# Attention's output weights loaded ahead in two DMAs each, and other loads moved later

## The chip, the cores and the metric

The kernel runs on one core of a Trainium2 chip. The metric is the device time of one execution in microseconds. Of the kernel before, three runs gave 2224.09, 2224.7 and 2230.74 us, a median of 2224.7 us. Engines are called TensorE (PE), VectorE (DVE), ScalarE (ACT), GpSimd (POOL) and SyncE (SP, whose queue issues all the DMAs spoken of here).

## The reference

One layer of a hybrid encoder over 2048 tokens of width 1024, in float32:

```python
h = rms_norm(x, norm1)
z = h @ w_in                       # q: 8 heads, k and v: 2 heads of 64, u: 512 columns
att = windowed_gqa(q, k, v, ...)   # QK norm, window of +-128 tokens, ALiBi, a sink logit per head
ssm = s5_mixer(u, ...)             # bidirectional complex diagonal scan, 32 groups; then GELU and GLU
x = x + concat([att, ssm]) @ w_out
x = x + square(relu(rms_norm(x, norm2) @ w_ff1)) @ w_ff2
```

`w_out` has 1024 rows. The upper 512 multiply the attention's result, and only these are loaded by the lines that the change touches. Attention works on blocks of 128 queries, each against its own block of keys and its two neighbours.

## The kernel before

Matrix products that need more precision are made of three: each operand is split into a rounded part and a rest (`woh` and `wol` for the output weights, `ah` and `al` for attention's result), and high x high, high x low and low x high are summed. So each weight tile needs a DMA into a raw tile, a copy on ScalarE that rounds it (L990), and a subtraction on VectorE (L991).

The program has these stages: (a) norm, transposes and the product for u, to about 139 us; (b) the products for q and k, v (`pq`, `pk`, in 16 tiles of 128 tokens, in pairs whose transposed inputs `hh` and `hl` are loaded by L898); (c) attention from about 349 to 720 us; (d) GLU, output projection of the state space part, second norm; (e) the two feed-forward products, from about 960 us on. Beside (b) and (c) runs the state space work as a second stream of steps (`ssm_stream`), in 8 sets of 4 groups: `ssm_load` brings a set's input `u` in 16 DMAs (L572), `pair_in` multiplies it (`ptv`, `pvu`), `ssm_rotate`, `ssm_scan` and `ssm_unrotate` work on VectorE, `pair_out` makes a kernel table that goes out to memory (`ks` to `kd_dr`, L738 and L740) and comes back in another layout (`tt`, L747), and `pair_y` multiplies with it (`py`, L759 and L762). How many of its steps follow each step of the main stream is set by a fixed rate (`Side`).

After each tile of (b), the keys are transposed (`ptk`, L944), scaled and split into `k_hh` and `k_ll` (`late_k`, L946 and L947). These calls wait in a list `late` until the next tile is under way. The order of the tiles is 14, 15, 12, 13, 0 to 11, so the last two calls, for tiles 10 and 11, are made when (b) has ended, ahead of attention.

Attention has 32 units: a block of 128 queries by one of the two key heads. `front(u)` makes a unit's queries (`q_prep`: `ptq`, `qs`), scores (`pss`) and softmax; `back(u)`, three units later (LEAD = 3), transposes the probabilities (`ptp`, copied to `pT` by L1061), multiplies with v (`pv`) once per block, splits the result (`ah` L1075, `al` L1076) and makes the output product of the block before (`poa`). `load_wo` is called twice in each of the units 1 to 4 and does DMA, rounding and subtraction for one of 8 parts: head `hh` of the four in a group, and a half of the columns. A part's 128 partitions are 64 rows for each key head, so the source of its one DMA has the two key heads outermost. Its raw tile `woraw` shares 7 buffers with `pT`.

A scheduler puts each engine's instructions into a fixed order from the program's order, the dependences and its own model of times. An engine then works strictly in that order, and SyncE issues its DMAs so too: a DMA that waits for something holds up all that stand behind it.

Of the kernel before, what the change touches and what calls it, by code (L numbers as in the profile page):

```python
# [11 lines left out]
F32 = mybir.dt.float32  # L12
# [8 lines left out]
P = 128  # L21
# [5 lines left out]
NKV = 2  # L27
GQ = 4
HD = 64
AW = 512  # L30
# [14 lines left out]
PTB = 7  # L45
# [12 lines left out]
def hymba_kernel(ctx: ExitStack, tc: tile.TileContext, x, norm1, w_in, q_gain, k_gain, sink,  # L58
                 lam_re, lam_im, log_dt, b_re, b_im, c_re, c_im, d_skip, w_glu, w_out,
                 norm2, w_ff1, w_ff2, out):  # L60
    nc = tc.nc
# [504 lines left out]
    def ssm_load(i):  # L566
        u = pm2.tile([P, 4, NC_], F32, tag="u", name="u")
        for g in range(4):
            for q in range(4):
                src = u_dr[q, (4 * i + g) * GH:(4 * i + g + 1) * GH]  # L570
                rows = bass.AP(src.tensor, src.offset, [[64, T], [T * 64, GH], [1, 64]])
                nc.sync.dma_start(out=u[:, g, q * 64:(q + 1) * 64], in_=rows)  # L572
        st[i] = {"u": u}
# [197 lines left out]
    NB4 = NG // 4  # L771

    def ssm_stream():
        ssm_load(0)
        yield from pair_in(0, 0)
        yield from pair_in(0, 1)
        yield from ssm_tables(0)
        for i in range(NB4):
            if i + 1 < NB4:
                ssm_load(i + 1)  # L780
            yield from ssm_rotate(i)
            yield from pair_out(i, 0)
            yield from ssm_scan(i)
            yield from ssm_unrotate(i)
            yield from pair_y(i, 0)
            if i + 1 < NB4:
                yield from pair_in(i + 1, 0)
            yield from pair_out(i, 1)
            if i + 1 < NB4:
                yield from pair_in(i + 1, 1)  # L790
                yield from ssm_tables(i + 1)
            else:
                for _ in range(8):
                    yield
            yield from pair_y(i, 1)
            del st[i]
# [84 lines left out]
    side = Side(side_stream(), SIDE_STEPS, SIDE_MAIN)  # L881


    with tc.tile_pool(name="p1", bufs=2) as p1:
        gq = p1.tile([P, 2], F32, name="gq", bufs=1)
        for j, gain in enumerate((q_gain, k_gain)):
            for r in range(2):
                nc.sync.dma_start(out=gq[r * HD:(r + 1) * HD, j:j + 1], in_=gain.rearrange("o d -> d o"))
        DVE.tensor_tensor(gq[:, 0:1], gq[:, 0:1], gq[:, 1:2], op=ALU.mult)
        hsc = p1.tile([P, 10], F32, name="hsc", bufs=1)  # L890
        DVE.memset(hsc, 1.0)
        for h in range(NH):
            DVE.memset(hsc[:, h:h + 1], -1.0 / (SLOPE[h] * math.sqrt(HD)))

        def load_h(b):
            for j, v in enumerate(ht_tiles(b)):
                for t in range(2):
                    nc.sync.dma_start(out=v.bitcast(F32)[:, :, t * P:(t + 1) * P],  # L898
                                      in_=ht_dr[2 * b + t, j].rearrange("p (k t) -> p k t", k=KD))

        def qkv_part(t):
            hh, hl = (a[:, :, (t % 2) * P:(t % 2) * P + P] for a in ht[t // 2])
            pq = ps.tile([P, 512], F32, tag="sc", name="pq")
            pk = ps.tile([P, 256], F32, tag="mm", name="pk")
            for k in range(KD):
                mm3(pq, hh[:, k, :], hl[:, k, :], wqh[:, k, 0:512], wql[:, k, 0:512], k == 0, k == KD - 1)
                yield 0.65
            for k in range(KD):
                mm3(pk, hh[:, k, :], hl[:, k, :], wqh[:, k, 512:768], wql[:, k, 512:768], k == 0, k == KD - 1)
                if k % 2:  # L910
                    yield 0.65
            pq3 = pq.rearrange("p (h d) -> p h d", d=HD)
            pk3 = pk[:, 0:128].rearrange("p (h d) -> p h d", d=HD)
            sq = p1.tile([P, 10, HD], F32, tag="sq", name="sq", bufs=1)
            ACT.activation(out=sq[:, 0:8], in_=pq3, func=AF.Square)
            ACT.activation(out=sq[:, 8:10], in_=pk3, func=AF.Square)
            ACT.activation(out=v_all[:, t, :], in_=pk[:, 128:256], func=AF.Copy)
            ms = p1.tile([P, 10], F32, tag="msq", name="msq")
            rs = p1.tile([P, 10], F32, tag="rsq", name="rsq")
            t3 = p1.tile([P, 10], F32, tag="t3", name="t3")  # L920
            DVE.tensor_reduce(ms, sq, axis=AX.X, op=ALU.add)
            DVE.tensor_scalar(ms, ms, 1.0 / HD, EPS, op0=ALU.mult, op1=ALU.add)
            ACT.activation(out=rs, in_=ms, func=AF.Sqrt)
            DVE.reciprocal(rs, rs)
            DVE.tensor_tensor(t3, rs, rs, op=ALU.mult)
            DVE.tensor_tensor(t3, t3, ms, op=ALU.mult)
            DVE.tensor_scalar(t3, t3, -0.5, 1.5, op0=ALU.mult, op1=ALU.add)
            DVE.tensor_tensor(rs, rs, hsc, op=ALU.mult)
            DVE.tensor_tensor(rs, rs, t3, op=ALU.mult)
            yield 0.0  # L930
            rs3 = rs.rearrange("p (h o) -> p h o", o=1)
            DVE.tensor_tensor(sq[:, 0:8], pq3, rs3[:, 0:8].to_broadcast([P, 8, HD]), op=ALU.mult)
            qd = p1.tile([P, NH, 2, HD], F32R, tag="qd", name="qd", bufs=1)
            kd = p1.tile([P, 2, 2, HD], F32, tag="kd", name="kd", bufs=3)
            for r in range(2):
                DVE.tensor_tensor(kd[:, :, r, :], pk3, rs3[:, 8:10].to_broadcast([P, 2, HD]), op=ALU.mult)
            ACT.activation(out=qd[:, :, 0, :], in_=sq[:, 0:8], func=AF.Copy)
            DVE.tensor_tensor(qd[:, :, 1, :], sq[:, 0:8], qd[:, :, 0, :], op=ALU.subtract)
            nc.sync.dma_start(out=q_dr[t], in_=qd.bitcast(F32).rearrange("p h r d -> p (h r d)"))

            def late_k():
                pt = ps.tile([P, 2, P], F32, tag="tr", name="ptk")
                for kv in range(2):
                    nc.tensor.transpose(pt[:, kv, :], kd[:, kv].rearrange("p r d -> p (r d)"), ident)  # L944
                ts_ = slice(t * P, (t + 1) * P)
                ACT.activation(out=k_hh[:, :, ts_], in_=pt, func=AF.Copy, scale=gq[:, 0:1])  # L946
                DVE.scalar_tensor_tensor(k_ll[:, :, ts_], pt, gq[:, 0:1], k_hh[:, :, ts_],  # L947
                                         op0=ALU.mult, op1=ALU.subtract)

            late.append(late_k)  # L950

        late = []
        order = [NB - 1, NB - 2] + list(range(NB - 2))
        for i, b in enumerate(order):
            for t in (2 * b, 2 * b + 1):
                if t % 2 == 0 and 1 <= i < NB - 1:
                    load_h(order[i + 1])
                for j, c in enumerate(qkv_part(t)):
                    side.step(c * FIRST)
                    if j == 4 and len(late) > 1:  # L960
                        late.pop(0)()
        while late:
            late.pop(0)()
    hstack.close()
    wqkv.close()

# [1 line left out]
    with tc.tile_pool(name="pbq", bufs=2) as pbq, tc.tile_pool(name="pb", bufs=1) as pb, \  # L968
# [4 lines left out]
        def load_q(n):  # L973
            qt = pbq.tile([P, NH, P], F32R, tag="qraw", name="qraw")
            nc.sync.dma_start(out=qt.bitcast(F32), in_=q_dr[n].rearrange("p (h r) -> p h r", h=NH))
            q_raw[n] = qt

        nc.sync.dma_start(out=nsink, in_=sink[0:1, :].to_broadcast([P, NH]))
        DVE.tensor_scalar(nsink, nsink, -1.0, None, op0=ALU.mult)
        load_q(0)  # L980
        load_q(1)
        woh = pb.tile([P, GQ, D], F32R, name="woh")
        wol = pb.tile([P, GQ, D], F32R, name="wol")

        def load_wo(hh, half):
            cs = slice(half * 512, half * 512 + 512)
            raw = pb.tile([P, 512], F32, tag="pT", name="woraw", bufs=PTB)
            src = w_out[0, 0:AW, cs].rearrange("(g hh d) n -> hh g d n", g=NKV, hh=GQ)
            nc.sync.dma_start(out=raw, in_=src[hh])
            ACT.activation(out=woh[:, hh, cs], in_=raw, func=AF.Copy)  # L990
            DVE.tensor_tensor(wol[:, hh, cs], raw, woh[:, hh, cs], op=ALU.subtract)  # L991

# [104 lines left out]
            yield 0.65  # L1097

        wo_parts = [(hh, half) for half in range(2) for hh in range(GQ)]

        def front(u):

            n, g = divmod(u, 2)
            for h in range(GQ):
                scores(n, g, h)
                if h == GQ - 1:
                    softmax(n, g)
                yield 0.33
                if h % 2 and u > 0 and wo_parts:
                    load_wo(*wo_parts.pop(0))  # L1110
                if h == 1 and u + 1 < 2 * NT:
                    q_prep(*divmod(u + 1, 2))
                    if g == 0 and n + 2 < NT:
                        load_q(n + 2)
                    yield 0.44
# [448 lines left out]
```

## Time and profile before

| | us |
|---|---|
| median of three runs | 2224.7 |
| the profiled execution, its own time | 2234.64 |
| its span | 2232.9 |
| TensorE busy | 2084.3 (93%) |
| VectorE busy | 1478.7 (66%) |
| ScalarE busy | 1016.1 (46%) |
| GpSimd busy | 591.5 (26%) |

TensorE is busy nearly throughout, so time is lost where it is not, or where its granted clock is below 1. The page's 40 slices of 55.8 us show three such places: the seventh slice (335 to 391 us, the change from stage (b) to attention), the seventeenth (893 to 949 us, the output projection) and the twenty-ninth (1563 to 1619 us, the change to the second feed-forward product). The DMA engines move 151 GB/s on average.

### The profile page before, as it was taken

How to read it: one execution, taken by the hardware profiler on the slowest of the kernel's cores; microseconds unless marked ns; L12 is line 12 of the kernel's file. 1: busy time of each engine (PE TensorE's matmuls, PEld its weight loads, DVE VectorE, ACT ScalarE, POOL GpSimd, SP SyncE). 2: the span in 40 equal slices, each digit the busy share in tenths (PEclk: the TensorE clock that was granted, in tenths of full speed). 3: DMA queues.
4: the chain of work that ended last, by engine and by line, in shares of the span. 5: the costliest groups of instructions: out<-in, count | busy, mean ns of one | idle time of the engine just before them, and what ended most of it. 6: DMA issues, size and time to landing. Idle time of an engine off the chain costs nothing.

```text
span 2232.9 us, 30461 instructions
## 1 busy us (share of the span) xinstructions
PE 2084.3 (93%) x10546; PEld 1710.8 (77%) x10546; DVE 1478.7 (66%) x2806; ACT 1016.1 (46%) x2061; POOL 591.5 (26%) x451
## 2 busy tenths in 40 slices
PE   7999995899999998699999999999599999999999
PEld 7888884677776776588888788888477787778787
DVE  7869876788775644565555655554677767776765
ACT  4433324677666532455555655555332332333331
POOL 2000000000002223232222122222554653663541
PEclk9999997999999999699999999999799999999999
DMA  9834543233326355844444644443573443443334
GB/s 257 284 90 135 158 127 110 90 107 102 109 83 184 118 203 193 274 154 153 156 156 156 217 156 156 154 149 112 199 242 115 128 131 101 128 128 107 125 130 163
DMA packets 284154, 337.06 MB, mean 151 GB/s; under 512 B 62688, under 2 KB 211168, under 8 KB 284000
## 3 DMA queue, kind: packets, MB, share of 16 engines
q1 hardware_dynamic: 284000, 335.12, 46.3%
q8 instruction: 83, 1.36, 0.3%
q14 instruction: 71, 0.58, 0.1%
HBM read 206.11 MB, written 128.94 MB: 150 GB/s over the span
## 4 chain that ended last, share of the span: by engine, by line
PE 63%; DVE 15%; DMA 8%; POOL 5%; issue 4%; ACT 3%; SPq 2%; DVEq 0%; POOLq 0%; ACTq 0%
PE f L87 6%; PE f L89 6%; PE f L88 6%; PE f_al L87 5%; PE f_al L89 5%; PE f_al L88 5%; POOL w2s L1452 3%; PE f_ga L89 2%; PE f_ga L87 2%; PE f_ga L88 2%; POOL fs L1478 1%; PE pv L1069 1%; DMA woraw<-in_w_out_dram 1%; DVE acc L1523 1%; PE f_be L88 1%
## 5 line engine op out<-in xcount | busy, mean ns | idle before, releaser
L1523 DVE TENSOR_TENSOR acc<-f,acc 128x512 f32<-128x512 f32 x448 | 304.9, 687 | 162.0 <-PE f L89 155.3
L87 PE MATMUL f<-w2s,fs 128*128 128x512 f32 x896 | 352.3, 393 | 30.5 <-DVE acc L1523 15.9
L89 PE MATMUL f<-w2s,fs 128*128 128x512 f32 x896 | 350.2, 391 | 4.9 <-POOL fs L1478 4.9
L88 PE MATMUL f<-w2s,fs 128*128 128x512 f32 x896 | 349.9, 391 | 0.0
L1477 ACT ACTIVATE fs<-fr 128x512 fp32r<-128x512 f32 x224 | 141.6, 633 | 363.1 <-PE f L89 344.9
L1478 POOL TENSOR_TENSOR fs<-fr,fs 128x512 fp32r<-128x512 f32 x128 | 185.4, 1451 | 295.8 <-ACT fs L1477 247.8
L87 PEld LDWEIGHTS f<-w2s,fs 128*128 128x128 f32 x896 | 169.0, 189 | 73.7 <-ACT fs L1477 26.3
L1321 POOL TENSOR_TENSOR w1s<-w1r,w1s 128x512 fp32r<-128x512 f32 x96 | 135.4, 1411 | 310.6 <-ACT w1s L1320 305.1
L87 PE MATMUL f_al<-hb,w1s 128*128 128x512 f32 x512 | 201.0, 393 | 0.7 <-ACT w1s L1320 0.7
L89 PE MATMUL f_al<-hb,w1s 128*128 128x512 f32 x512 | 200.7, 392 | 0.9 <-DVE w1s L1321 0.8
L88 PE MATMUL f_al<-hb,w1s 128*128 128x512 f32 x512 | 200.4, 392 | 0.0
L89 PEld LDWEIGHTS f<-w2s,fs 128*128 128x128 f32 x896 | 168.9, 189 | 41.1 <-POOL fs L1478 5.6
L88 PEld LDWEIGHTS f<-w2s,fs 128*128 128x128 f32 x896 | 169.1, 189 | 34.4
L818 POOL TENSOR_TENSOR wgl<-wgr,wgh 128x512 fp32r<-128x512 f32 x8 | 10.4, 1317 | 555.2 <-DMA wgr<-in_w_glu_dram 542.4
L1321 DVE TENSOR_TENSOR w1s<-w1c,w1s 128x512 fp32r<-128x512 f32 x96 | 68.3, 711 | 87.9 <-ACT w1s L1320 87.9
L89 PEld LDWEIGHTS f_al<-hb,w1s 128*128 128x128 f32 x512 | 96.5, 189 | 21.9 <-DVE w1s L1321 1.2
L87 PEld LDWEIGHTS f_al<-hb,w1s 128*128 128x128 f32 x512 | 96.7, 189 | 21.0 <-ACT w1s L1320 1.1
L88 PEld LDWEIGHTS f_al<-hb,w1s 128*128 128x128 f32 x512 | 96.6, 189 | 19.5
L1320 ACT ACTIVATE w1s<-w1c 128x512 fp32r<-128x512 f32 x128 | 80.6, 630 | 49.6 <-PE f_al L89 48.4
L88 PE MATMUL f_ga<-hb,w1s 128*128 128x512 f32 x256 | 99.9, 390 | 0.0
L87 PE MATMUL f_ga<-hb,w1s 128*128 128x512 f32 x256 | 99.8, 390 | 0.0
L89 PE MATMUL f_ga<-hb,w1s 128*128 128x512 f32 x256 | 99.7, 389 | 0.0
(548 smaller groups left out, 4975.3 us busy)
## 6 DMA issues: line engine op xcount, KB each, us to landing
fr<-f_dr SPq DMA_DIRECT2D x224, 256.0 KB
w1r<-in_w_ff_dram SPq DMA_DIRECT2D x64, 512.0 KB
f_dr<-fs SPq DMA_DIRECT2D x128, 256.0 KB
f_dr<-f SPq DMA_DIRECT2D x96, 256.0 KB
w2r<-in_w_ff_dram SPq DMA_DIRECT2D x32, 512.0 KB
hs<-hc_dr SPq DMA_DIRECT2D x56, 256.0 KB
xt<-in_x_dram SPq DMA_DIRECT2D x16, 512.0 KB
q_dr<-qd SPq DMA_DIRECT2D x16, 512.0 KB
```

The source lines that it names most:

```text
L87: nc.tensor.matmul(ps_ap, lhsT=lh, rhs=rh, start=first, stop=False, skip_group_check=onto)
L88: nc.tensor.matmul(ps_ap, lhsT=lh, rhs=rl, start=False, stop=False, skip_group_check=onto)
L89: nc.tensor.matmul(ps_ap, lhsT=ll, rhs=rh, start=False, stop=last, skip_group_check=onto)
L818: eng_lo.tensor_tensor(lo, raw, hi, op=ALU.subtract)
L1069: nc.tensor.matmul(po[g * HD:(g + 1) * HD, :], lhsT=v_all[:, lo + kt, g * HD:(g + 1) * HD], rhs=pT.pop((n, g, kt)), start=kt == 0, stop=kt ...
L1320: ACT.activation(out=t[:, 0], in_=src, func=AF.Copy)
L1321: (DVE if m in (6, 7, 3) else POOL).tensor_tensor(t[:, 1], src, t[:, 0], op=SUB)
L1452: (DVE if m in (6, 7, 3) and fp else POOL).tensor_tensor(t[:, 1], src, t[:, 0], op=SUB)
L1477: ACT.activation(out=t[:, 0], in_=src, func=AF.Copy)
L1478: (DVE if m in (6, 7, 3) else POOL).tensor_tensor(t[:, 1], src, t[:, 0], op=SUB)
L1523: DVE.tensor_tensor(a[:, cs], po, a[:, cs], op=ADD)
```

## The change

The diff, whole:

```diff
--- before.py
+++ after.py
@@ -776,11 +776,11 @@
         yield from pair_in(0, 1)
         yield from ssm_tables(0)
         for i in range(NB4):
-            if i + 1 < NB4:
-                ssm_load(i + 1)
             yield from ssm_rotate(i)
             yield from pair_out(i, 0)
             yield from ssm_scan(i)
+            if i + 1 < NB4:
+                ssm_load(i + 1)
             yield from ssm_unrotate(i)
             yield from pair_y(i, 0)
             if i + 1 < NB4:
@@ -881,8 +881,11 @@
     side = Side(side_stream(), SIDE_STEPS, SIDE_MAIN)
 
 
+    late_stack = ExitStack()
+    with tc.using_default_side("right"):
+        lk = late_stack.enter_context(tc.tile_pool(name="lk", bufs=1))
     with tc.tile_pool(name="p1", bufs=2) as p1:
-        gq = p1.tile([P, 2], F32, name="gq", bufs=1)
+        gq = lk.tile([P, 2], F32, name="gq")
         for j, gain in enumerate((q_gain, k_gain)):
             for r in range(2):
                 nc.sync.dma_start(out=gq[r * HD:(r + 1) * HD, j:j + 1], in_=gain.rearrange("o d -> d o"))
@@ -931,7 +934,7 @@
             rs3 = rs.rearrange("p (h o) -> p h o", o=1)
             DVE.tensor_tensor(sq[:, 0:8], pq3, rs3[:, 0:8].to_broadcast([P, 8, HD]), op=ALU.mult)
             qd = p1.tile([P, NH, 2, HD], F32R, tag="qd", name="qd", bufs=1)
-            kd = p1.tile([P, 2, 2, HD], F32, tag="kd", name="kd", bufs=3)
+            kd = lk.tile([P, 2, 2, HD], F32, tag="kd", name="kd", bufs=3)
             for r in range(2):
                 DVE.tensor_tensor(kd[:, :, r, :], pk3, rs3[:, 8:10].to_broadcast([P, 2, HD]), op=ALU.mult)
             ACT.activation(out=qd[:, :, 0, :], in_=sq[:, 0:8], func=AF.Copy)
@@ -959,8 +962,6 @@
                     side.step(c * FIRST)
                     if j == 4 and len(late) > 1:
                         late.pop(0)()
-        while late:
-            late.pop(0)()
     hstack.close()
     wqkv.close()
 
@@ -975,18 +976,23 @@
             nc.sync.dma_start(out=qt.bitcast(F32), in_=q_dr[n].rearrange("p (h r) -> p h r", h=NH))
             q_raw[n] = qt
 
+        load_q(0)
         nc.sync.dma_start(out=nsink, in_=sink[0:1, :].to_broadcast([P, NH]))
         DVE.tensor_scalar(nsink, nsink, -1.0, None, op0=ALU.mult)
-        load_q(0)
-        load_q(1)
         woh = pb.tile([P, GQ, D], F32R, name="woh")
         wol = pb.tile([P, GQ, D], F32R, name="wol")
 
+        wo_raw = {}
+
         def load_wo(hh, half):
-            cs = slice(half * 512, half * 512 + 512)
             raw = pb.tile([P, 512], F32, tag="pT", name="woraw", bufs=PTB)
-            src = w_out[0, 0:AW, cs].rearrange("(g hh d) n -> hh g d n", g=NKV, hh=GQ)
-            nc.sync.dma_start(out=raw, in_=src[hh])
+            src = w_out[0, 0:AW, half * 512:half * 512 + 512].rearrange("(g hh d) n -> hh g d n", g=NKV, hh=GQ)
+            for g in range(NKV):
+                nc.sync.dma_start(out=raw[g * HD:(g + 1) * HD], in_=src[hh][g])
+            wo_raw[hh, half] = raw
+
+        def split_wo(hh, half):
+            raw, cs = wo_raw.pop((hh, half)), slice(half * 512, half * 512 + 512)
             ACT.activation(out=woh[:, hh, cs], in_=raw, func=AF.Copy)
             DVE.tensor_tensor(wol[:, hh, cs], raw, woh[:, hh, cs], op=ALU.subtract)
 
@@ -1097,6 +1103,12 @@
             yield 0.65
 
         wo_parts = [(hh, half) for half in range(2) for hh in range(GQ)]
+        for part in wo_parts[:4]:
+            load_wo(*part)
+        load_q(1)
+        for part in wo_parts[4:PTB]:
+            load_wo(*part)
+        late_wo = wo_parts[PTB:]
 
         def front(u):
 
@@ -1106,8 +1118,14 @@
                 if h == GQ - 1:
                     softmax(n, g)
                 yield 0.33
-                if h % 2 and u > 0 and wo_parts:
-                    load_wo(*wo_parts.pop(0))
+                if h % 2 and u > 1 and wo_parts:
+                    split_wo(*wo_parts.pop(0))
+                    if late_wo:
+                        load_wo(*late_wo.pop(0))
+                if h == 2 and u > 0 and late:
+                    late.pop(0)()
+                    if not late:
+                        late_stack.close()
                 if h == 1 and u + 1 < 2 * NT:
                     q_prep(*divmod(u + 1, 2))
                     if g == 0 and n + 2 < NT:
```

It has these parts.

1. `load_wo` only issues DMAs now, two for each part (64 partitions each, one per key head). Seven parts, as many as there are buffers, are asked for ahead of unit 0, the eighth after the first split.
2. `split_wo` does the rounding and the subtraction, twice in each of the units 2 to 5 instead of 1 to 4.
3. The last two `late_k` are made in units 1 and 2 of attention. What they read (`kd` and the gains `gq`) moves into a pool of its own that lives until then.
4. `ssm_load` of the next set is called after `ssm_scan` instead of ahead of `ssm_rotate`.
5. `load_q(0)` stands ahead of the sink's load, and `load_q(1)` between the fourth and the fifth weight part.

What the scheduler makes of it: the orders differ from the first of the `u` loads (139 us in the trace) to the last third of attention; from there to the end all engines have the same order as before.

SyncE at the start of attention, before (`tt`: the state space table, `qraw`: a block's queries, `xr`: the input rows for the residual):

```order
L747 DMA tt<-kd_dr 128x1x384
L975 DMA qraw<-q_dr 128x1024
L989 DMA woraw<-in_w_out_dram 128x1x512 x3
L975 DMA qraw<-q_dr 128x1024
L989 DMA woraw<-in_w_out_dram 128x1x512
L1084 DMA xr<-in_x_dram 128x1024
L989 DMA woraw<-in_w_out_dram 128x1x512 x4
L975 DMA qraw<-q_dr 128x1024
```

and now:

```order
L747 DMA tt<-kd_dr 128x1x384 x2
L976 DMA qraw<-q_dr 128x1024
L991 DMA woraw<-in_w_out_dram 64x512 x16
L976 DMA qraw<-q_dr 128x1024
L1090 DMA xr<-in_x_dram 128x1024
L976 DMA qraw<-q_dr 128x1024
```

The first weight DMA stands at the same place, behind the third block of queries; the eight are now sixteen, without a gap, and the fourth block of queries and `xr` come behind all of them. The last two of the sixteen wait for the first split's buffer.

SyncE in the state space work of the second set, while the third set's `u` is loaded (`y_dr`: a result stored, `hh`, `hl`: inputs of the next pair of tiles, `kd_dr`: the table stored), before:

```order
L768 DMA y_dr<-ys 8x16x256 x2
L572 DMA u<-u_dr 128x1x64 x16
L898 DMA hh<-ht_dr 128x8x128 x2
L939 DMA q_dr<-qd 128x1024
L898 DMA hl<-ht_dr 128x8x128 x2
L738 DMA kd_dr<-ks 16x256
L740 DMA kd_dr<-ks 16x240
L738 DMA kd_dr<-ks 16x256
L740 DMA kd_dr<-ks 16x240
L747 DMA tt<-kd_dr 128x1x384
```

and now:

```order
L768 DMA y_dr<-ys 8x16x256 x2
L572 DMA u<-u_dr 128x1x64 x7
L901 DMA hh<-ht_dr 128x8x128 x2
L901 DMA hl<-ht_dr 128x8x128 x2
L738 DMA kd_dr<-ks 16x256
L740 DMA kd_dr<-ks 16x240
L942 DMA q_dr<-qd 128x1024
L738 DMA kd_dr<-ks 16x256
L740 DMA kd_dr<-ks 16x240
L747 DMA tt<-kd_dr 128x1x384
L572 DMA u<-u_dr 128x1x64 x3
L747 DMA tt<-kd_dr 128x1x384
```

Nine of the sixteen `u` loads have moved from ahead of the table's stores to behind its first reload, and a store of queries stands between the table's stores.

TensorE at the start of attention, before (`pkd`: the state space table's product):

```order
L726 MATMUL pkd<-q_n,f_i_1814 32x256 x2
L730 MATMUL pkd<-c_r,bb_r 16x16 x2
L730 MATMUL pkd<-c_n,bb_i 16x16 x2
L944 MATMUL ptk<-ident,kd 128x128 x4
L1008 MATMUL ptq<-ident,qraw 128x128 x5
L1023 MATMUL pss<-k_hh,qs 128x256
```

and now:

```order
L726 MATMUL pkd<-q_n,f_i_1814 32x256 x2
L730 MATMUL pkd<-c_r,bb_r 16x16 x2
L730 MATMUL pkd<-c_n,bb_i 16x16 x2
L1014 MATMUL ptq<-ident,qraw 128x128 x8
L1029 MATMUL pss<-k_hh,qs 128x256
```

The four key transposes ahead of the first query transposes are gone; two of them now stand behind the scores of the first unit and two among the scores of the third.

## Rows read from the trace of the kernel before

**Rows 1.** The page: span, and TensorE's granted clock in 40 slices, in tenths.
```profile
span 2232.9 us, 30461 instructions
...
PEclk9999997999999999699999999999799999999999
```
**Rows 2.** Stretches of the opening: length, PE, PEld, DVE, ACT, POOL busy, PEclk, DMA share, GB/s.
```profile
371.00:413.00 42.00, 18.29 (x89) 12.48 (x90) 17.47 (x52) 19.28 (x51) 0.00 (x0) 0.67 0.23 76
356.70:406.20 49.50, 24.51 (x108) 17.12 (x109) 22.11 (x80) 25.11 (x65) 0.00 (x0) 0.67 0.32 99
356.70:368.50 11.80, 11.56 (x62) 9.82 (x63) 6.28 (x32) 6.89 (x16) 0.00 (x0) 0.78 0.52 143
413.00:443.00 30.00, 28.03 (x181) 22.60 (x182) 29.55 (x82) 24.78 (x70) 0.00 (x0) 1.00 0.31 92
```
**Rows 3.** Chain of work that ended last, in order of time: start, length, what.
```profile
378.38 15.45 DMA woraw<-in_w_out_dram
...
395.23 15.01 DMA woraw<-in_w_out_dram
```
**Rows 4.** Waits, 345 to 420 us: who waited for whom, us in total, times, longest.
```profile
ACT woh L990 <- DMA woraw<-in_w_out_dram: 22.6, 8, 4.7
...
PE ptq L1008 <- ACT pT L1061: 17.1, 1, 17.1
```
**Rows 5.** ScalarE's groups, 356.7 to 406.2 us: busy, mean ns, idle before them.
```profile
L990 ACT ACTIVATE woh<-woraw 128x512 fp32r<-128x512 f32 x7 | 4.4, 629 | 18.5 <-DMA woraw<-in_w_out_dram 18.5
L1010 ACT ACTIVATE qs<-ptq 128x512 fp32r<-128x512 f32 x6 | 3.6, 595 | 5.3 <-PE ptq L1008 4.5 <-PE pss L1024 0.8
```
**Rows 6.** DMA engines from 378 to 388 us, in 40 slices of 0.25 us.
```profile
DMA  1111935699944111111111111111111111101111
GB/s 49 49 49 49 279 98 180 229 360 393 377 180 180 49 49 49 49 49 49 49 49 49 49 49 49 49 49 49 49 49 49 49 49 49 66 33 66 49 49 41
```
**Rows 7.** The opening in order of time: start, length, engine, instruction, idle before it.
```profile
348.43 0.33 SPq L975 DMA_DIRECT2D qraw<-q_dr  x1
...
355.17 0.66 PE L944 MATMUL ptk<-ident,kd 128*128 128x128 f32 x2 [5.32 <-DVE kd L936]
...
356.72 0.60 ACT L1010 ACTIVATE qs<-ptq 128x512 fp32r<-128x512 f32 x1 [0.38 <-PE ptq L1008]
...
361.12 4.46 SPq L989 DMA_DIRECT2D woraw<-in_w_out_dram  x3
...
405.56 0.59 ACT L1075 ACTIVATE ah<-pv 128x512 fp32r<-128x512 f32 x1
...
413.33 0.48 PE L87 MATMUL poa<-woh,ah 128*128 128x512 f32 x1
```
**Rows 8.** SyncE's queue in the state space groups, in order of time.
```profile
208.24 9.81 SPq L572 DMA_DIRECT2D u<-u_dr  x16
...
223.63 2.25 SPq L738 DMA_DIRECT2D kd_dr<-ks  x1
...
229.33 0.62 SPq L747 DMA_DIRECT2D tt<-kd_dr  x1
...
284.09 0.62 SPq L747 DMA_DIRECT2D tt<-kd_dr  x1
```
**Rows 9.** TensorE in the same two groups.
```profile
229.81 1.06 PE L637 MATMUL pvu<-u,vt 128*128 128x128 f32 x8
...
233.71 0.71 PE L759 MATMUL py<-u,tt 128*128 128x128 f32 x4 [1.47 <-DMA tt<-kd_dr]
...
288.49 1.22 PE L759 MATMUL py<-u,tt 128*128 128x128 f32 x4 [4.00 <-DMA tt<-kd_dr]
```
**Rows 10.** Two stretches of the second group, columns as in rows 2.
```profile
280.00:290.00 10.00, 5.79 (x34) 4.96 (x33) 4.47 (x14) 2.85 (x7) 0.00 (x0) 0.84 0.53 155
290.00:300.00 10.00, 10.00 (x67) 9.22 (x68) 4.86 (x8) 1.41 (x4) 0.00 (x0) 0.82 0.13 36
```
**Rows 11.** Issues on SyncE by tile: least, median and longest ns, first and last start.
```profile
L572 SPq DMA_DIRECT2D u<-u_dr x128: 567/574/707, 139.2 to 559.2; - x128
```

## The prediction, made before the changed kernel was run

> **What bounds the kernel now.** I read the page first, then the opening of attention in stretches, then the chain of waits, the waits by engine, the DMA rate, and last SyncE's queue in the state space work. The page gives a span of 2232.9 us, and TensorE is busy for most of it; one of the three places where its granted clock is below full level is the seventh slice, where attention begins [rows 1]. There TensorE is busy for only 18.29 of the 42 us from 371 to 413, at a mean clock of 0.67, a mixture of the two levels of 1.2 and 2.4 GHz, and from 413 on it is busy for 28.03 of 30 at 1.00 [rows 2]. So some 24 us are lost in this one stretch, and nothing in it is bound by an engine: ScalarE has 19.28 us of work, VectorE 17.47.
>
> The chain of waits names what ends last there: two pieces of about 15 us each are DMAs of `woraw` [rows 3]. ScalarE, which works strictly in its order, waits for them 8 times, 22.6 us in all; while it stands before one rounding, the copies of transposed probabilities queue behind it, and TensorE waits 17.1 us for one of these [rows 4]. Of the 22.6 us, 18.5 fall ahead of `ah`, the first split result of attention [rows 5], and 4.1 between `ah` at 405.56 and the first output product at 413.33 [rows 7].
>
> Why are the loads so slow? In most slices where only they run, the engines move 49 GB/s and are busy for one tenth; when `xr` joins, the same engines reach 393 GB/s [rows 6]. One part is 128 rows of 2 KB, 262 KB, and 262 KB / 49 GB/s = 5.3 us. So a part's DMA uses about a tenth of the engines; its source has the two key heads outermost, and the DMA that runs beside it has not.
>
> **The weights (parts 1 and 2 of the change).** The same eight roundings and eight subtractions are made; only what ScalarE waits for goes. The first weight DMA keeps its place behind the third block of queries, at 361.1 before [rows 7], some 3 us earlier now (next part). Sixteen issues at the median of a `u` issue, 0.574 us [rows 11], are 9.2 us, so the seventh part is issued by about 366. A transfer of 131 KB at 180 to 393 GB/s [rows 6] takes 0.3 to 0.7 us, about an issue, and from issue to use I allow the 4.4 us that `tt` took (229.33 to 233.71) [rows 8, 9]. All seven parts are there by 371. The first rounding now stands behind the second unit's exponentials, and ScalarE was through the first unit's only at about 368.5, so none of the seven is waited for. The eighth waits for the first subtraction; behind it SyncE holds the fourth block of queries and `xr`, both first used more than 15 us later. Taken away: 22.6 us.
>
> What comes late instead? ScalarE's order, and what feeds it. From the first `qs` at 356.72 to `ah` it has 25.11 us of work in 49.5 [rows 2]; without the 18.5 us it would need 31. Work added to it there: the two `k_hh` copies, at most 0.6 us each, since `qs` with twice the columns takes 0.595 [rows 5]: +1.2. Waits that surface: between 368.5 and 406.2 its work is 25.11 - 6.89 = 18.2 us. At the pace of the first 11.80 us, in which no weights are waited for (4.91 us idle on 6.89 of work), this would bring 13 us of waits; at the pace of 413 to 443 (5.22 on 24.78) 3.8; with perfect overlap none [rows 2]. I take 4, since the stretch has the same mixture of two units at work as the steady state. VectorE, with 22.11 us in the opening, has room.
>
> A rule speaks against splitting the DMA. The Trainium skill (DMA: Bandwidth & Descriptors, section Rules for kernel authors) says that two transfers to disjoint halves of the partitions are not worth it, since both run over all 16 engines and serialize. By it the split would bring nothing, which is a rival below. The same page (section Why a DMA increments its semaphore by 16 and not by 1) lets the number of engines be the largest up to 16 that divides the slowest dimension of both sides: 2 for the old source, 16 for each of the new ones, and the sum would be as here. The trace's tenth of the engines is nearer to the second.
>
> **The key transposes (part 3).** TensorE's first query transposes stand behind those of the last tile, which wait 5.32 us for VectorE's `kd` [rows 7]. Now they stand first and wait for their own data, asked for at 348.43. With 4.4 us from issue to use they start at 352.8 instead of 355.6: -2.8. Ends: 0, if the queries land later than that, and -5.3, the whole wait. The scores of block 0 read neither tile; the moved transposes take places in units 1 and 2, where TensorE waits anyway.
>
> **The state space loads (part 4).** The third set's 16 `u` issues hold SyncE from 208.24 for 9.81 us; the table's store follows at 223.63 and its reload at 229.33 [rows 8]. TensorE waits 1.47 us for that table, and 4.00 us for the next set's at 288.49 [rows 9], after which its clock is 0.84 and 0.82 over 20 us [rows 10]. Nine issues fewer ahead of the table are 9 x 0.574 = 5.2 us. Best end: both waits (5.5) and what the clock lost (0.16 + 0.18 of 10 us each, 3.4): -8.9. Worst end: TensorE's order has also moved `py` ahead, by up to 8 us, and a query store stands between the table's stores, so a new wait of 3 us is possible: +3. I take -3, the middle: the larger wait goes, and a smaller new one comes in another set.
>
> **Clock.** The output products now start while TensorE has just been half idle; before, it had been busy from 400 on. Five of their first microseconds at the low level cost 2.5; between -2 (the opening itself at a higher level) and +4 I take +1.5. The reordered `load_q` and the sink's load wait for nothing that binds: 0; the eight more issues lie in SyncE's queue beside 25 us of ScalarE's work: 0.
>
> **Sum**: -22.6 + 1.2 + 4 - 2.8 - 3 + 1.5 = -21.7 us. The profiled execution took 2234.64, so 2212.9 for such a one; that is 9.9 above the median of the runs, and no view tells where. Against the median, 2224.7 - 21.7 = 2203.0.
>
> **Rivals.**
> - The opening stays chained (13 us of waits surface, not 4): +9, 2212. For it: the idle share of the first 11.80 us, and the low clock makes each link through TensorE longer. Against: 413 to 443. Chance 0.14.
> - The DMAs stay narrow, by the rule above: 5.3 us each for a part, from about 358. The eighth part lands at 401 instead of 410, so the first output product moves from 413 to about 404; with the rest of the sum, -10: 2215. For it: nothing in the rows; against: 393 GB/s. Chance 0.08.
> - More goes than I count: no surfaced wait (-4) and the best end for the table (-6): 2193. For it: the low clock [rows 10] may go with the wait ahead of it. Chance 0.12.
> - Slower: the `u` loads come too late. Half of a set's `u` is needed by `pvu`, at 229.81 in the third set [rows 9]; its eighth DMA now stands behind the first table reload, about 229.3 - 5.2 = 224.1, and lands by 229 at 4.4 us. That is a margin of under 1 us. If it is lost in each of the six sets that follow by over (21.7 + 6.7) / 6 = 4.7 us, the kernel is slower: 2232 or more. Against: TensorE's order has put `pvu` later too. Chance 0.03.
> - A wait takes the place of the one removed: the weights now hold all seven buffers, and the copies of transposed probabilities wait for subtractions instead, so TensorE's 17.1 us [rows 4] stay: -4.6, 2220. Against: those subtractions need only what is loaded. Chance 0.03.
>
> **How the numbers follow.** The forecast's own case, 2196 to 2211, has chance 0.60. The measurement cannot tell less than 0.3%, 6.7 us, from no change. The first four cases are faster by more than that, except where the narrow DMAs come out short: 0.92; within it 0.05; slower 0.03. The range 2194 to 2214 leaves out half of the largest gain, the narrow DMAs, the kept wait and the slower case.
>
> **What would show it.** Right: weight DMAs at over 150 GB/s; no wait of ScalarE on `woraw` over 1 us; first output product at 389 to 396 on the old scale; `ptk` no longer ahead of the first `ptq`; less wait for `tt` in stage (b). Wrong: 49 GB/s again; `ah` still over 40 us behind the first `qs`; `pvu` waiting for `u`; a table wait of over 3 us.

## The result and the profile after

The changed kernel takes 2200.5 us (median of 4 runs, 2198.6 to 2201.4) against 2227.7 for the kernel before in the same session (4 runs, 2224.1 to 2231.6): a ratio of 0.9865 with a 95% interval of 0.9848 to 0.9883. The forecast was 2203.0 with a range of 2194 to 2214. In the experiments' sessions the kernel before had medians of 2224.8, 2228.7 and 2226.0, so by medians the gain is 24 to 28 us (27.2 in its own session); by the ratio, which is not the quotient of the two medians (0.9878), it is 30 us (26 to 34).

The page of the changed kernel, span and TensorE's granted clock, to be set beside [rows 1]:

```profile
span 2198.4 us, 30479 instructions
...
PEclk9999999999999999799999999999799999999999
```

The two profiled spans differ by 34.5 us. The seventh slice is back at 9 tenths or more. The seventeenth reads a tenth higher; the slices cut the program elsewhere now, but over the same piece of it (893 to 949 us before, 857 to 913 now), whose order of instructions did not change, the mean clock is 0.68 and 0.76. Lines of the changed kernel are numbered higher than those of before (`ah` is L1081, `woh` L996, `wol` L997). The opening of attention in order of time, which answers to [rows 7]:

```profile
345.13 0.33 SPq L976 DMA_DIRECT2D qraw<-q_dr  x1
...
348.58 1.06 PE L1014 MATMUL ptq<-ident,qraw 128*128 128x128 f32 x8 [2.41 <-DMA qraw<-q_dr]
...
349.52 0.58 ACT L1016 ACTIVATE qs<-ptq 128x512 fp32r<-128x512 f32 x1
...
353.82 12.01 SPq L991 DMA_DIRECT2D woraw<-in_w_out_dram  x16
...
380.58 0.60 ACT L1081 ACTIVATE ah<-pv 128x512 fp32r<-128x512 f32 x1 [0.45 <-PE pv L1075]
...
384.17 0.48 PE L87 MATMUL poa<-woh,ah 128*128 128x512 f32 x1
```

Four landmarks divide the 34.5 us. The first query load is issued 3.3 us earlier (345.13 for 348.43). From there to `qs` it takes 4.4 us instead of 8.3: 3.9 gained. From `qs` to `ah`, 31.1 instead of 48.8: 17.8 gained. From `ah` to the first output product, 3.6 instead of 7.8: 4.2 gained. From the first output product to the end, 1814.2 instead of 1819.6: 5.3. These add up to the whole. The two outer pieces, 3.3 and 5.3, are no more than the spread between traces: in the 14 traces of this document the first query load is issued at 342.9 to 348.7 us, and the last piece takes 1809.8 to 1819.6, the longest being that of the kernel before. The three inner ones, 25.9, are the change's.

What became of the waits is in the tile `woraw` of the changed kernel (count, least, median and longest ns, first and last start):

```profile
L991 SPq DMA_DIRECT2D woraw<-in_w_out_dram x16: 465/594/597, 353.8 to 365.2; - x16
L996 ACT ACTIVATE woh<-woraw x8: 613/632/644, 362.9 to 382.1; 128x512 fp32r<-128x512 f32 x8
L997 DVE TENSOR_TENSOR wol<-woraw,woh x8: 682/685/693, 364.0 to 386.3; 128x512 fp32r<-128x512 f32 x8
its engine sat idle before it (us, times) until:
  ACT woh L996: 1.0, 1
```

ScalarE no longer waits for a weight DMA; in [rows 4] it was 22.6 us. And the rate while they run, 355 to 362 us, against the 49 GB/s of [rows 6]:

```profile
DMA  8799989698999999879898999899999996554595
GB/s 278 260 348 351 296 170 246 152 322 231 234 281 222 164 187 164 187 176 281 176 246 141 222 211 187 164 234 234 281 269 234 246 222 152 129 140 141 176 269 152
```

What sets the opening now? First the stretch from `qs` to `ah` of the changed kernel, then ten microseconds of it (columns as in [rows 2]):

```profile
349.50:380.60 31.10, 22.84 (x131) 17.28 (x130) 22.60 (x78) 25.85 (x70) 0.00 (x0) 0.89 0.59 166
360.00:370.00 10.00, 3.31 (x15) 2.94 (x16) 5.67 (x20) 9.97 (x32) 0.00 (x0) 0.75 0.84 253
```

ScalarE does 25.85 us of work in 31.1, and from 360 to 370 it never stops. TensorE stands in that time, and the list of waits names something else for it:

```profile
PE ptp L1065 <- DVE k_ll L950: 5.5, 1, 5.5
```

This is one of the moved key transposes. Whether the transposes cost these 5.5 us or only stand behind ScalarE, the list can't say; experiment 9 can.

### The profile page after: what moved, and what is told of

The parts are those of the page before. It is cut to its first block, busy times and chain, and to the rows that moved or that the text cites. A ratio compares the mean times of both kernels' runs of the same rounds, so it can differ in the third digit from the quotient of the medians.

```text
span 2198.4 us, 30479 instructions
## 1 busy us (share of the span) xinstructions
PE 2077.8 (95%) x10546; PEld 1706.7 (78%) x10546; DVE 1479.6 (67%) x2806; ACT 1016.0 (46%) x2061; POOL 590.3 (27%) x451
## 4 chain that ended last, share of the span: by engine, by line
PE 67%; DVE 13%; DMA 7%; POOL 5%; issue 3%; ACT 3%; SPq 1%; DVEq 0%; POOLq 0%; ACTq 0%
PE f L87 6%; PE f L89 6%; PE f L88 6%; PE f_al L89 5%; PE f_al L87 5%; PE f_al L88 5%; PE f_ga L87 3%; PE f_ga L89 3%; PE f_ga L88 3%; POOL w2s L1470 2%; PE pv L1075 1%; POOL fs L1496 1%; PE ptp L1065 1%; DVE acc L1541 1%; PE f_be L89 1%
## 5 line engine op out<-in xcount | busy, mean ns | idle before, releaser
L89 PEld LDWEIGHTS f<-w2s,fs 128*128 128x128 f32 x896 | 169.7, 189 | 40.3 <-POOL fs L1496 4.5
L1339 DVE TENSOR_TENSOR w1s<-w1c,w1s 128x512 fp32r<-128x512 f32 x96 | 68.3, 711 | 88.0 <-ACT w1s L1338 88.0
```

The source lines that it names most:

```text
L89: nc.tensor.matmul(ps_ap, lhsT=ll, rhs=rh, start=False, stop=last, skip_group_check=onto)
L1339: (DVE if m in (6, 7, 3) else POOL).tensor_tensor(t[:, 1], src, t[:, 0], op=SUB)
```

## The experiments

Each kernel was timed beside the kernel before, in 5 rounds. "Opening" is the time in the trace from the issue of the first query load to the first output product, "stage end" the time of that issue. Experiments 1 to 4, 5 to 8 and 9 to 12 are three sessions on three chips, and their ratios rest on different runs of before.

| kernel | median us | ratio to before (95%) | stage end | opening |
|---|---|---|---|---|
| before | 2224.8 to 2228.7 | 1 | 348.4 | 64.9 |
| changed | 2200.5 | 0.9865 (0.9848 to 0.9883) | 345.1 | 39.0 |
| 1 split alone | 2202.6 | 0.9897 (0.9879 to 0.9915) | 345.7 | 44.9 |
| 2 cut by columns | 2230.2 | 1.0021 (1.0006 to 1.0035) | 342.9 | 68.3 |
| 3 ahead, not split | 2220.6 | 0.9982 (0.9971 to 0.9992) | 345.8 | 61.4 |
| 4 weights only | 2209.9 | 0.9921 (0.9903 to 0.9940) | 348.7 | 42.2 |
| 5 changed, keys back | 2202.3 | 0.9880 (0.9862 to 0.9898) | 343.5 | 40.3 |
| 6 changed, loads back | 2203.4 | 0.9887 (0.9869 to 0.9906) | 345.1 | 42.3 |
| 7 changed, not ahead | 2200.4 | 0.9870 (0.9853 to 0.9888) | 345.2 | 40.1 |
| 8 changed, GpSimd rounds | 2201.0 | 0.9866 (0.9844 to 0.9889) | 345.9 | 39.0 |
| 9 changed, keys in units 6, 7 | 2198.1 | 0.9877 (0.9862 to 0.9892) | 346.9 | 39.2 |
| 10 both of 8 and 9 | 2200.4 | 0.9883 (0.9869 to 0.9897) | 344.7 | 41.5 |
| 11 loads alone | 2222.5 | 0.9986 (0.9974 to 0.9997) | 343.4 | 62.4 |
| 12 keys alone | 2225.5 | 1.0000 (0.9989 to 1.0011) | 345.4 | 63.4 |

**1. The split alone**, on the kernel before:

```diff
-            nc.sync.dma_start(out=raw, in_=src[hh])
+            for g in range(NKV):
+                nc.sync.dma_start(out=raw[g * HD:(g + 1) * HD], in_=src[hh][g])
```

> The kernel before, with each weight part fetched by one DMA per key head; nothing is asked for earlier, no order is changed. Theory W (the width of the DMA makes the wait): a part arrives in about 1 us instead of 5.3, the rate in the opening rises from 49 to over 150 GB/s, ScalarE's waits on woraw fall from 22.6 to under 8 us, and the time from 2227.7 to 2207 to 2213 us. Theory A (being asked for ahead makes the gain, the width does little): each part still costs its whole way from issue to use, 3 to 4 us, so ScalarE still waits 15 us or more: 2219 to 2227 us.

Measured 0.9897, beyond even the stronger expectation. The tile `woraw` of this kernel, issues and roundings, and ScalarE's only wait for it:

```profile
L990 SPq DMA_DIRECT2D woraw<-in_w_out_dram x16: 465/586/597, 357.9 to 390.1; - x16
L991 ACT ACTIVATE woh<-woraw x8: 612/615/634, 365.8 to 393.3; 128x512 fp32r<-128x512 f32 x8
...
ACT woh L991 <- DMA woraw<-in_w_out_dram: 0.2, 1, 0.2
```

Nothing is asked for ahead, and of 22.6 us of waits 0.2 are left: SyncE's queue runs ahead of ScalarE by itself once its DMAs are short (first issue at 357.9, first rounding at 365.8). These two lines alone give 22 to 23 us (medians 22.2 apart, 0.0103 by the ratio).

**2. As many DMAs, cut by columns**, on the kernel before:

```diff
-            nc.sync.dma_start(out=raw, in_=src[hh])
+            for c in (0, 256):
+                nc.sync.dma_start(out=raw[:, c:c + 256], in_=src[hh][:, :, c:c + 256])
```

> The kernel before, with each weight part fetched by two DMAs, as in the first experiment, but cut by columns: each still has the two key heads outermost in its source and brings half the columns (1 KB rows). As many DMAs and bytes as there. Theory W (what limits the rate is the outermost dimension of two): 49 GB/s or little more, ScalarE's waits on woraw stay at 18 to 25 us, 2222 to 2232 us. Rival (it is the number of DMAs in flight that limits): 100 GB/s or more and half the wait, 2208 to 2217 us.

The first expectation holds: 1.0021. ScalarE's wait in this kernel, and the DMA engines from 372 to 378 us:

```profile
ACT woh L991 <- DMA woraw<-in_w_out_dram: 23.1, 7, 5.2
...
DMA  2111111111111111111110111111011111119523
GB/s 61 61 41 48 48 41 48 48 41 41 48 48 41 41 48 48 41 48 61 48 55 27 55 55 55 55 55 48 21 55 48 48 41 48 41 48 212 96 96 102
```

Two DMAs bring no more per second than one, as long as each has the two heads outermost. So it is neither the number of DMAs nor their size. The rows of 1 KB instead of 2 change nothing either; what is left is the outermost dimension. Other sizes of it than two and 64 were not run.

**3. Asked for ahead, not split**, on the changed kernel: the two DMAs of `load_wo` are one again, as in the first diff read backwards.

> The changed kernel, with each weight part fetched by one DMA as in the kernel before (asked for ahead, roundings from the third unit on, keys and state space loads late as changed). Theory W with DMAs one behind the other at 5.3 us: the seventh part lands at about 391 instead of 366, ScalarE waits for parts 5 to 8 some 10 us in all, first output product little later, attention 6 to 13 us longer: 2206 to 2214 us (the rival named in the prediction said 2215). Theory A (being ahead is enough): 2199 to 2204 us, no wait on woraw of over 1 us.

Measured 0.9982, 2220.6: slower than either theory said; of the whole gain 4 us are left. SyncE's queue and ScalarE's wait in this kernel:

```profile
354.24 27.95 SPq L990 DMA_DIRECT2D woraw<-in_w_out_dram  x7
382.29 5.14 SPq L976 DMA_DIRECT2D qraw<-q_dr  x1
...
ACT woh L995 <- DMA woraw<-in_w_out_dram: 24.2, 7, 5.0
```

Seven issues hold SyncE for 27.95 us (the shortest of the eight takes 0.52, the longest 7.40), where sixteen split ones take 12.01. The parts come 5.3 us apart, which is 262 KB at 49 GB/s: ScalarE starts the third, fourth and fifth rounding at 375.02, 380.36 and 385.71. So asking ahead does not hide the narrow DMAs here, and the queue is not free meanwhile: the next query load behind the seven takes 5.14 us to issue. In the kernel before, the longest of the eight issues took 5.56 us.

**4. The weights only** (ahead and split), keys and loads in their old places.

> The changed kernel with the last key transposes back ahead of attention and each state space load back ahead of the rotation: of the change only the weights (and the order of the first query loads) are left. Theory W by the terms of the prediction: the keys are worth 2.8 and the loads 3 us, so 2205 to 2208 us. Rival K (the keys carry more, since with them the opening stays dense): over 2209 us. Rival N (both are hidden anyway): 2199 to 2203 us.

The median is 2209.9, but of two kinds: four runs at 2209.9 to 2210.5, where rival K had its number, and two at 2201.8 and 2203.6, about where rival N had its own. The trace is of one of the four and does not bear K's reason out: the opening stays dense without the moved keys. It is 2.8 us shorter than with the split alone, but its stage end is 3.1 us later, and from the first output product to the end it takes 5.5 us more (2208.1 - 390.9 against 2202.3 - 390.6). TensorE's granted clock is 0.94 from 470 to 500 us there, where the first experiment has 1.00. What makes this one program take two times some 7 us apart stays open.

**5 and 6. Keys back, loads back**, each on the changed kernel:

```diff
+        while late:
+            late.pop(0)()
...
+                ssm_load(i + 1)
             yield from ssm_rotate(i)
```

> The changed kernel (0.9865 of before) with the last key transposes back ahead of attention. Theory W+K: the transposes cost the start their place and a wait for kd, in the two traces 7.2 against 3.45 us from the first query load's issue to the first query transpose, so 3 to 4 us (2.8 in the prediction): 0.9878 to 0.9884 of before. Rival: the keys are hidden elsewhere, since in the changed kernel they make TensorE wait 5.5 us for k_ll in the opening: 0.985 to 0.987. Rival K (the keys are what keeps the opening dense): over 0.990.

> The changed kernel (0.9865 of before) with each state space load back ahead of the rotation. The prediction's term: 3 us of table waits and clock come back, 0.9876 to 0.9882 of before. Rival (spread): in traces of the same old order the state space stage ended at 348.43, 345.69, 342.94 and 348.74 us, and with the new order at 345.13 and 345.77, so the 3.3 us seen are run to run spread and the loads are worth under 1 us: 0.986 to 0.987.

0.9880 and 0.9887, that is 0.0015 and 0.0022 (3.3 and 4.9 us) more than the changed kernel, where the prediction's terms were 2.8 and 3. The fifth lies in its first range, the sixth above both of its ranges. With intervals of 0.002 to either side neither is told from nothing by the runs; the quotients of the medians are only 0.0003 and 0.0009 more. The traces say where. With the keys back the opening is 1.3 us longer. With the loads back the stage end is the same, 345.09, and the opening is 3.3 us longer. Its start there, and what answers to it in the changed kernel (`msq` is VectorE's first step for the last tile's queries and keys, `qd` a later one on ScalarE):

```profile
345.09 0.33 SPq L976 DMA_DIRECT2D qraw<-q_dr  x1
...
347.74 0.81 DVE L924 TENSOR_REDUCE msq<-sq 128x10 f32<-128x640 f32 x1
...
351.09 0.63 ACT L940 ACTIVATE qd<-sq 128x512 fp32r<-128x512 f32 x1 [2.09 <-DVE sq L935]
351.63 1.06 ACT L1016 ACTIVATE qs<-ptq 128x512 fp32r<-128x512 f32 x2
...
352.26 0.58 PE L1029 MATMUL pss<-k_hh,qs 128*128 128x256 f32 x1 [2.03 <-ACT qs L1016]
```

```profile
345.44 0.82 DVE L924 TENSOR_REDUCE msq<-sq 128x10 f32<-128x640 f32 x1 [0.18 <-ACT sq L919]
...
348.99 0.63 ACT L940 ACTIVATE qd<-sq 128x512 fp32r<-128x512 f32 x1 [1.98 <-DVE sq L935]
```

With the loads back VectorE comes to `msq` straight from state space work, 2.65 us behind the first query load instead of 0.31. ScalarE's `qd` waits for what follows from it, the first `qs` stands behind `qd`, and TensorE waits for `qs`. The second block of queries is issued 1.9 us later there too (350.33 for 348.44), but TensorE does not wait for it. Why VectorE is less far behind with the loads moved was not followed further.

**7. Not ahead**: the changed kernel, each part asked for where it is rounded, from the second unit on.

> The changed kernel (0.9865 of before), but each weight part is asked for where it is rounded, from the second unit on as in the kernel before, by one DMA per key head; keys and state space loads stay late. It leaves only the asking ahead out. Theory W (width is the gain): from first query transpose to first output product 37.4 us with the split alone in place, 35.2 and 35.6 asked ahead, so 2 us: 0.987 to 0.9878 of before. Theory A (the asking ahead carries a third or more of the gain): over 0.990.

0.9870, the first expectation's lower end: with the DMAs split, asking ahead shortens the opening from 40.1 to 39.0 us in the traces, and the runs don't tell it from nothing.

**8. GpSimd rounds and subtracts**, on the changed kernel, directly behind each load:

```diff
-            ACT.activation(out=woh[:, hh, cs], in_=raw, func=AF.Copy)
-            DVE.tensor_tensor(wol[:, hh, cs], raw, woh[:, hh, cs], op=ALU.subtract)
+            POOL.tensor_copy(woh[:, hh, cs], raw)
+            POOL.tensor_tensor(wol[:, hh, cs], raw, woh[:, hh, cs], op=ALU.subtract)
...
```

> The changed kernel (0.9865 of before) with the eight roundings and subtractions of the output weights on GpSimd, which has nothing else in this stretch, each directly behind its load. ScalarE loses 8 times 0.63 us = 5 us in the opening, VectorE 8 times 0.68 = 5.5 us. Theory S (in the changed kernel ScalarE's work sets the opening: busy 9.97 of 10 us from 360 to 370): first output product 3 to 5 us earlier, 0.984 to 0.9855 of before. Rival (GpSimd's traffic slows VectorE, or the chain through TensorE and VectorE takes over): 0.986 to 0.989.

**9 and 10. The key transposes in units 6 and 7** (`u > 5` for `u > 0`), alone and with GpSimd.

> The changed kernel (0.9865 of before) with the last two key transposes in units 6 and 7 instead of 1 and 2, behind the opening. Theory S (ScalarE's work sets the opening, busy 9.97 of 10 us from 360 to 370; TensorE's 5.5 us wait for k_ll only shows it): the two copies of 0.46 us leave the opening, nothing else, 0.9855 to 0.9868 of before. Rival (the transposes stand ahead of the first transposes of probabilities, so their wait is on the path): 2 to 5 us, 0.984 to 0.9855.

> Both of the last two ideas: roundings and subtractions of the output weights on GpSimd, key transposes in units 6 and 7. On GpSimd alone TensorE still waited 7.9 us for k_ll, and the time did not move (0.9866). If ScalarE and the key transposes held the opening together, it is now 4 to 8 us shorter: 0.983 to 0.985 of before. Rival (the chain of scores, VectorE and exponentials alone holds it): 0.9855 to 0.987.

By the ratio none of the three beats the changed kernel (0.9866, 0.9877 and 0.9883 against 0.9865), and none of the openings is shorter (39.0, 39.2 and 41.5 us against 39.0). The eighth is where its rival was; the ninth and the tenth lie above all their ranges, though their intervals reach into the upper ones. In the ninth the wait for `k_ll` is gone, and another has its place; ScalarE still works through:

```profile
PE pss L1029 <- ACT b_r L639: 5.8, 1, 5.8
...
360.00:370.00 10.00, 3.60 (x28) 3.06 (x26) 6.02 (x27) 9.99 (x35) 0.00 (x0) 0.93 0.71 185
```

So the 5.5 us wait only showed ScalarE's queue. But to take 5 us of work from ScalarE does not help either. VectorE's groups from 360 to 378 us, the changed kernel first, then the eighth:

```profile
L1031 DVE CUSTOM_DVE_ANT_0 p<-pss,dist 128x384 f32<-128x384 f32 x5 | 2.8, 553 | 1.0 <-PE pss L1030 1.0
L1054 DVE TENSOR_SCALAR p<-p,rc 128x256 f32<-128x256 f32 x4 | 1.2, 348 | 0.0
L1054 DVE TENSOR_SCALAR p<-p,rc 128x384 f32<-128x384 f32 x2 | 0.8, 418 | 0.0
...
L564 DVE TENSOR_TENSOR tmp<-b_i,t_s 128x512 f32<-128x512 f32 x1 | 0.7, 685 | 0.0
```

```profile
L1031 DVE CUSTOM_DVE_ANT_0 p<-pss,dist 128x384 f32<-128x384 f32 x8 | 4.2, 548 | 0.5 <-PE pss L1030 0.5
L1054 DVE TENSOR_SCALAR p<-p,rc 128x256 f32<-128x256 f32 x4 | 3.9, 1011 | 0.0
L1054 DVE TENSOR_SCALAR p<-p,rc 128x384 f32<-128x384 f32 x2 | 1.9, 965 | 0.0
L564 DVE TENSOR_TENSOR b_i<-b_i,t_c 128x512 f32<-128x512 f32 x1 | 1.8, 1770 | 0.0
```

The scaling of the probabilities takes 2.3 to 2.9 times as long while GpSimd works, and it stands in the chain from exponentials to transposes. From 349.5 to 380 us VectorE is busy for 24.97 us instead of 22.00, although its seven subtractions there (4.8 us) are gone. So a part of what ScalarE gave, VectorE lost. `ah` comes 29.3 us behind the first `qs` instead of 31.1, but the first output product 5.3 behind `ah` instead of 3.6, with more state space products ahead of it in TensorE's order. What sets the opening now stays open: it did not shorten without the early key transposes, without ScalarE's eight roundings, or without both.

**11 and 12. Loads alone, keys alone**, on the kernel before.

> The kernel before with each state space load behind the scan, nothing else. The prediction's term (the table waits of the state space stage): 3 us, 0.998 to 0.9992 of before. Rival (in that stage the spread covers it; what the loads hold up is the second block of queries at the start of attention, issued at 350.33 instead of 348.44 with the loads back in the changed kernel, and here the narrow weight DMAs hide that): 0.9993 to 1.0007.

> The kernel before with the last two key transposes in units 1 and 2, nothing else. The prediction's term: attention starts 2.8 us earlier (3.7 by the two traces), and the weight DMAs with it, 0.998 to 0.9992 of before. Rival (the waits for the weights take it back): 0.9993 to 1.001.

The loads give 0.9986, 3.1 us (0.7 to 5.8), as the prediction's term said, although the narrow weight DMAs are still there; the interval's end, 0.9997, only just reaches the rival's range. The keys give nothing without the rest (1.0000), although the first `qs` comes 6.2 us behind the first query load instead of 8.3. TensorE's wait list in that kernel's opening says where the earlier start went:

```profile
PE ptp L1060 <- DVE k_ll L950: 16.2, 1, 16.2
```

The kernel before waited these us at `ptq` [rows 4]; TensorE still stands behind the same weights, for which ScalarE waits 20.7 us here.

## Why the prediction was right, step by step

- **What bounds the opening**: shown. The narrow DMAs did (experiments 1 to 3). Asking for each part only where it is rounded cost little (7). The prediction treated the split and the asking ahead as one step; the runs give nearly all of this step to the split.
- **The two rules of the Trainium skill.** Splitting changed the rate from 49 GB/s to 219 on average (355 to 362 us), so what the Trainium skill (DMA: Bandwidth & Descriptors, section Rules for kernel authors) says of two transfers to disjoint halves did not hold for this source. What the Trainium skill says on the same page of the slowest dimension (section Why a DMA increments its semaphore by 16 and not by 1), two engines for the old source, agrees with experiment 2 and with the engines' mean busy share of 0.13, two of sixteen, from 365 to 370 us of experiment 3, where only narrow DMAs run.
- **-22.6 of waits**: right; 18.5 ahead of `ah` and 4.1 behind it went entirely (17.8 and 4.2 net).
- **+1.2 of added copies**: right; the two copies took 0.46 us each, and all of ScalarE's work from `qs` to `ah` is 25.85 us; before it was 24.56 (25.11 in [rows 2], less the part of `ah` itself), so 1.3 more.
- **+4 of waits that surface**: mis-sized, the largest error. ScalarE is idle for 5.25 us of the 31.1. Before, it was idle for 24.3 up to `ah`, 18.5 of them for weights [rows 5], so 5.8 were left: the waits that surfaced come to -0.6. Of the three paces the prediction had, the end for perfect overlap was the nearest.
- **-2.8 for the keys**: mis-sized, and a term of the loads was missing beside it. From the first query load to the first `qs` the traces gain 3.9 (8.3 to 4.4 us), but not by the keys alone. It takes 8.0 to 8.6 us where neither is moved (before, 1, 2, 4), 6.2 and 6.5 with the keys moved (12, 6), 5.7 and 6.3 with the loads moved (5, 11), and 4.4 to 4.5 in the six traces with both. So the keys make 1.6 to 2.0 of it and the loads 2.0 to 2.4, which the prediction put at nothing here. In all 14 traces VectorE's last `msq` starts 2.2 to 2.8 us behind the first query load in the old order of loads, and 0.3 to 0.4 in the new. Whether the keys are worth anything in the time, experiments 5 and 12 do not tell.
- **-3 for the loads**: the size agrees (3.1 us alone, 0.7 to 5.8), the place is wrong at least in part. TensorE's whole wait for `tt` in the state space stage was 7.3 us before (3.6 to 6.4 in the other traces of that order) and is 4.5 now, with 3.5 us of new waits for VectorE at the same products:

```profile
PE py L759 <- DMA tt<-kd_dr: 4.5, 5, 2.4
...
PE py L759 <- DVE t L929: 2.0, 1, 2.0
PE py L759 <- DVE tmp L564: 1.5, 1, 1.5
```

  The stage ended at 342.9 to 348.7 us in six traces of the old order of loads and at 343.4 to 346.9 in eight of the new: means of 346.0 and 345.1. I had read one trace's 4.0 us wait and its low clock [rows 9, 10] as the kernel's; it was one end of a spread. Nor did the low clock all lie behind the wait, as I wrote: the wait ended at 288.49, and the first of the two stretches begins at 280. What the loads gave showed in the opening (6: 3.3 us; 11: 2.5 us).
- **+1.5 for the clock**: wrong in sign or nothing. From 360 to 380 it is 0.75 and 0.91 now, and from 384 to 400, where the output products start, it is 1.00.
- **The base**: against 2224.7 the change gave 24.2, against the median of its own session 27.2. The profiled run of before, 2234.6, was slower than the four timed ones; 5.3 us of the difference between the two profiles lie behind the first output product. From there to the last group of output products it was 301.2 us before and is 295.7 now, and 296.3 to 299.4 in the traces of the twelve experiments, whether the parts are split or not; what part of this is the change's stays open. That the forecast came within 2.5 us of 2200.5 is luck in part: the terms gave 21.7 us, the session's runs gave 27.2 by medians and 30 by the ratio, and the base of 2224.7 lay 3.0 below that session's median, 2227.7.
- **What was to show it**: rate, waits and key transposes came as said. The first output product came at 384.2, not at 389 to 396 (391.6 by the sum): the surfaced waits (4.6), the clock (1.5), the start (1.1) and the stage end (0.3) make the difference.
- **The rivals**: narrow DMAs, priced at 2215, would be 2220.6 (3). I had the eighth part landing at 401 and the first output product at 404; the eighth is rounded at 405.2, and the product starts at 407.2. I had counted the transfer, but not that SyncE is held for it; the eighth part is issued only at 388.1, behind a query load and `xr`. How much of the 5.6 us this makes is not shown. The `u` loads came in time: TensorE's waits for them are 0.8 us in both kernels. The chain of waits that surface (2212) and the kept wait (2220) did not come. Of the case in which more goes (2193) the first half came, no surfaced wait, and the table's half did not.

## What to carry to other kernels

When a load runs at an eighth of the rate that a neighbouring one reaches (49 and 393 GB/s), look at the outermost dimension of its two sides before moving it earlier: the split was worth 22 to 23 us, the earlier request about 1 (by the traces). Ask what a wait named in the profile stands behind before removing it (the `k_ll` wait), and what a relieved engine shares with the next one. And take a term from several traces where the program allows it: of one trace's waits, those that come and go by 3 us from run to run are no property of the kernel.

## What the runs showed of the hardware

- DMAs whose source has the two heads outermost move 49 GB/s and hold the queue that issues them. On SyncE the first two of a row of seven took 1.10 us together, the five behind them 3.7 to 7.4 us each and 5.3 on average (3), which is 262 KB at 49 GB/s; one of a single head's 64 rows takes 0.594 at the median. With half the bytes the median issue took 2.74 us (2), which is 131 KB at 48 GB/s. So once the first are under way, the queue issued these DMAs no faster than they moved.
- VectorE and GpSimd get in each other's way by operand. While GpSimd rounded and subtracted, VectorE's scaling in place went from 348 to 1011 ns, and a product of two operands in on-chip memory from 685 to 1770 (one instance each); the score step, which reads TensorE's result, kept its 553 (548). The Trainium skill (SBUF — State Buffer, section SBUF: two separate sides) says that the two engines share a pair of ports under an exclusive lock, taken for the whole instruction; the rows agree with it.
- One program can take two times in the same session (experiment 4, some 7 us apart), and four traces of the same order of instructions up to there (before, experiments 1, 2 and 4) end the state space stage 5.8 us apart.
